# A hybrid decoder layer on one Trainium2 core: the squares of the delta-rule outputs are taken four chunks at a time and summed by VectorE, and VectorE makes the last square of the final norm

## The chip, the core and the metric

The kernel runs on one core of a Trainium2 chip. Five engines take part, each working through its own instruction queue in order: TensorE (PE in the profile: matrix products and transposes; PEld is its weight load, which overlaps), VectorE (DVE), ScalarE (ACT), GpSimd (POOL) and SyncE (SP, which here only issues transfers). The metric is the device time of one execution in microseconds. Three runs of the kernel before gave 1201.8, 1201.89 and 1199.36 us, median 1201.8; the profiled execution took 1200.36 us.

## The reference, cut to what matters

One layer of a decoder over 1024 tokens of width 1024, all in float32.

```python
h = rmsnorm(x, norm1_w)
proj = h @ w_in                       # q, k, v, z of mixer A; q, k, v of mixer B
...                                   # mixer A: short convolution, L2-normed q and k
def step(state, xs):                  # over chunks of tokens, for each of 4 heads
    uv, wk, qd, at, ke, ge = xs
    u = uv - wk @ state
    o = qd @ state + at @ u
    state = ge * state + ke.T @ u
    return state, o
o_a = rmsnorm(o_a, gdn_norm_w) * silu(z)      # mean square over the 128 columns of a head
o_b = dilated_attention(qb, kb, vb)           # mixer B, 8 heads of 64
x = x + concat(o_a, o_b) @ w_out
...                                   # rmsnorm, up projection, width-3 convolution, silu gate
x = x + (silu(gate) * up) @ w_down
return rmsnorm(x, final_norm_w)
```

The two things the change touches are the mean square in `rmsnorm(o_a, ...)` (one number for each token and head) and a quarter of the last eighth of the mean square in the final `rmsnorm`.

## The kernel before

**Stages.** The program is written as coroutines ("streams") that yield to a small planner, the class `Weave`. The planner keeps an estimated clock of TensorE and an estimated time at which every tile is ready, worked out from fixed costs for each engine (VectorE 0.07 us plus 0.00105 us an element, ScalarE 0.12 plus 0.00085, and 0.15 more for a square with an accumulated sum). At each point it lets the ready stream of the smallest level number go on. The order in which matrix products are emitted is the order on TensorE. On the other engines a list scheduler sets the order: operations issued through `uv` and `ua` (VectorE and ScalarE, recorded on line 144) go ahead of those issued through `ve` and `ac` (line 142). Line 193 is the helper that issues a matrix product, line 197 the one that issues a transpose.

In order of time the stages are: input projection of the keys; preparation of the four delta-rule heads; the four chains (about 240 to 305 us); the attention (about 320 to 442 us); the output projection; the MLP up (to about 800 us) and down (to about 1189 us); the final norm (to the end). The dense input projection, `dense`, is a stream of low rank that is cut into groups of three products of 128x512 (`ps<-xhi,whi`, `ps<-xlo,whi`, `ps<-xhi,wlo`: a float32 product made of three products of rounded parts). It supplies TensorE with work wherever the planner sees the chains or the attention not ready, and does so until after the attention. So a product of it that is done earlier is missing later, but none is lost.

**A chain.** `chain(h)` runs the recurrence of one head over 8 chunks of 128 tokens; four chains are interleaved. In each chunk: TensorE makes `kT` times the state `ct`; VectorE makes `r`; TensorE makes `yt` times `r` (`ps<-r,um`); VectorE scales it to `wke` and ScalarE copies it to `w`; TensorE makes `ps<-wke,ktok`; VectorE updates the state `ct`; TensorE makes the output `po` out of `ct,qat` and `w,qat`; ScalarE and then VectorE write the output into `vtok` (`vtok<-ps,rq`, `vtok<-ps,gq,vtok`). Before the change ScalarE then squares the chunk's 128x128 outputs into a scratch tile `osq` and adds the squares of each token up on the way into one column of `ms` (the accumulated sum is a second instruction, ACTIVATION_READ_ACCUMULATOR). After the 8 chunks VectorE scales `ms` to a mean, GpSimd takes its power of minus one half and scales `vtok` by it, and `finish(h)` transposes `vtok` and stores it through the tile `ot` for the gate. Tiles `ot`, and later tiles of the attention and of the norms, share a ring of two buffers, tag "t2".

**The end.** The last five steps of the down product for four output tiles are made in `last_product`, first for columns 0 to 255 ("left"), then 256 to 511 ("right"). After each, `add_to` adds the product to `x1h` (VectorE), and `complete` squares the 128x256 result on ScalarE; all squares but the very last (`apart`) are added into `rstdB` by VectorE. `mean_of` sums over partitions with products against a column of ones, first from `rstdB`, then from the last square `sq3` (`sq` in the profile); GpSimd takes the power; `turned` spreads it by a transpose; `scale_out` scales the tiles and stores them. The scaling of left tiles 6 and 7 is tied behind the last addition on VectorE by a manual dependency.

Of the kernel before, what the change touches and what calls it, by code (L numbers as in the profile page):

```python
# [7 lines left out]
F32 = mybir.dt.float32  # L8
F32R = mybir.dt.float32r
AF = mybir.ActivationFunctionType  # L10
OP = mybir.AluOpType
AX = mybir.AxisListType
# [3 lines left out]
P = 128  # L16
# [131 lines left out]
def hybrid_layer(tc, I, out):  # L148
    nc = tc.nc
    wv = Weave()  # L150
    ve = Engine(wv, nc.vector, "vector", 0.07, 0.00105)
    ac = Engine(wv, nc.scalar, "scalar", 0.12, 0.00085)

    uv = Engine(wv, nc.vector, "vector", 0.07, 0.00105, first=tc.high_priority)
    ua = Engine(wv, nc.scalar, "scalar", 0.12, 0.00085, first=tc.high_priority)
# [7 lines left out]
    sp = es.enter_context(tc.tile_pool(name="sp", bufs=1))  # L163
# [3 lines left out]
    def tile_(pool, shape, dt, name, tag, bufs):  # L167
        return wv.slot(pool.tile(list(shape), dt, name=name, tag=tag, bufs=bufs), tag, bufs)
# [3 lines left out]
    def A(name, tag, dt=F32, shape=(P, 1024)):  # L172
        if tag in TURNS:
            i = turns[tag] = turns.get(tag, -1) + 1
            tag = TURNS[tag][i % len(TURNS[tag])]
        return tile_(lp, shape, dt, name, tag, SLOTS[tag])
# [15 lines left out]
    def mm(dst, lhs, rhs, us, start=True, stop=True, **kw):  # L192
        tc.stamp_issue_order_token(nc.tensor.matmul(dst, lhs, rhs, start=start, stop=stop, **kw).ins, TOKEN)  # L193
        wv.product(us, dst, lhs, rhs)
# [54 lines left out]
    def rsqrt(dst, src, n):  # L249
        po_.tensor_tensor(dst, src, mhalf[:, :n], op=OP.pow)  # L250
# [14 lines left out]
    def bank(tag, name="ps"):  # L265
        return tile_(pp_, (P, 512), F32, name, tag, 2)

    def next_bank(tag, *tiles, slack=0.0):

        while max(wv.need(*tiles), wv.slot_free(tag, 2)) + slack > 1e-3:  # L270
            yield max(wv.need(*tiles), wv.slot_free(tag, 2)) + slack
        return bank(tag)

    def half(i):
        return slice(i * 512, i * 512 + 512)

    def v8(t):
        return t.rearrange("p (c t) -> p c t", c=NCH)
# [239 lines left out]
    def small(name, bufs=2):  # L518
        return tile_(sp, (P, NCH), F32, name, name, bufs)
# [316 lines left out]
    def chain_load(h, s):  # L836
        t = A("qat", "go" if s == 1 and h < 2 else "qa", shape=(P, 2, 512))
        sy.dma_start(t[:, 0, :], qpark[h][:, half(s)])
        sy.dma_start(t[:, 1, :], atpark[h][:, half(s)])
        return t  # L840
# [3 lines left out]
    def chain(h):  # L844

        for i in range(H):
            yield from wv.until(("m", i))
            yield from wv.until(("v", i))
        d = G[h]
        kT, ktok, vtok, yt, ge, rq, gq, ke = [d[n] for n in ("kT", "ktok", "vtok", "yt", "ge", "rq", "gq", "ke")]  # L850
        if not ct:
            ct.append(A("ct", "uy", shape=(P, 8, P)))
        sts = ct[0][:, 2 * h:2 * h + 2, :]
        qa = chain_load(h, 0)
        ps = bank(("asc", "ch")[h // 2])
        ms = small("ms", 4)
        tg = str(h)
        st = None
        for c in range(NCH):
            cs = slice(c * P, (c + 1) * P)  # L860
            if c == 2 and h < 2:
                qb = chain_load(h, 1)
            if c == 3 and h >= 2:
                yield from wv.until(("c", h - 2, 3))
                qb = chain_load(h, 1)
            if c == 4:
                qa = qb
            qT, at = [qa[:, i, (c % 4) * P:(c % 4 + 1) * P] for i in range(2)]
            if c == 0:
                r = vtok[:, cs]  # L870
                yield wv.need(ps, vtok, yt)
            else:
                yield wv.need(ps, st, slack=HOP)
                mm(ps[:, 0:P], kT[:, cs], st, 0.215)
                r = tile_(sp, [P, P], F32, "r", "r" + tg, 1)
                uv.scalar_tensor_tensor(r, ps[:, 0:P], ngam[:, c, h:h + 1], vtok[:, cs], op0=OP.mult, op1=OP.add)
                yield wv.need(r, slack=HOP)
            mm(ps[:, P:2 * P], yt[:, c, :], r, 0.215)
            w = tile_(sp, [P, P], F32, "w", "w" + tg, 1)
            if c < NCH - 1:  # L880
                wke = tile_(sp, [P, P], F32, "wke", "r" + tg, 1)
                uv.tensor_scalar(wke, ps[:, P:2 * P], ke[:, c:c + 1], None, op0=OP.mult)
            ua.activation(w, ps[:, P:2 * P], AF.Copy)
            if c < NCH - 1:
                yield wv.need(wke, slack=HOP)
                mm(ps[:, 2 * P:3 * P], ktok[:, cs], wke, 0.215)
                sn = sts[:, c % 2, :]
                if c == 0:
                    uv.tensor_copy(sn, ps[:, 2 * P:3 * P])
                else:  # L890
                    uv.scalar_tensor_tensor(sn, st, ge[:, c:c + 1], ps[:, 2 * P:3 * P], op0=OP.mult, op1=OP.add)
            yield wv.need(w, qa, slack=HOP)
            po = yield from next_bank("atr")
            if c:
                mm(po[:, P:2 * P], qT, st, 0.215)
            mm(po[:, :P], at, w, 0.215)

            ua.activation(vtok[:, cs], po[:, :P], AF.Copy, scale=rq[:, c:c + 1])
            if c:
                uv.scalar_tensor_tensor(vtok[:, cs], po[:, P:2 * P], gq[:, c:c + 1], vtok[:, cs], op0=OP.mult,  # L900
                                        op1=OP.add)
            if c < NCH - 1:
                st = sn
            osq = tile_(sp, [P, P], F32, "osq", "osq", 1)
            ua.activation(osq, vtok[:, cs], AF.Square, accum_out=ms[:, c:c + 1])
            wv.done.add(("c", h, c))

        ve.tensor_scalar(ms, ms, 1.0 / 128, EPS, op0=OP.mult, op1=OP.add)
        rsqrt(ms, ms, NCH)
        po_.tensor_tensor(v8(vtok), v8(vtok), ms[:, :, None].to_broadcast([P, NCH, P]), op=OP.mult)  # L910
        wv.add(1, finish(h, vtok))

    def finish(h, osb):
        for hh in range(2):
            pt = yield from next_bank("atr", osb)
            for c in range(4):
                i = 4 * hh + c
                tp(pt[:, c * P:(c + 1) * P], osb[:, i * P:(i + 1) * P])
            ot = tile_(sp, [P, 512], F32, "ot", "t2", 2)
            ac.activation(ot, pt, AF.Copy, scale=gw2)  # L920
            sy.dma_start(mixer[h][:, half(hh)], ot)
        wv.done.add(("o", h))
# [589 lines left out]
    def part(m, hh, sl):  # L1512
        return slice(512 * hh + sl.start, 512 * hh + sl.stop)
# [6 lines left out]
    def complete(m, hh, sl, apart=False):  # L1520

        sp_ = part(m, hh, sl)
        x = x1h[m][:, sp_]
        sq = tile_(sp, [P, 512], F32, "sq3", "t2", 2)
        ac.activation(sq[:, sl] if m else rstdB[:, sp_], x, AF.Square)
        if apart:
            return sq
        if m:
            ve.tensor_tensor(rstdB[:, sp_], rstdB[:, sp_], sq[:, sl], op=OP.add)

# [38 lines left out]
    def mlp_down():  # L1569
# [4 lines left out]
        def down_step(stage, j):  # L1574
            for e, (op, pds) in enumerate(zip(ops[stage, j], (pa, pb))):
                for i in range(4):
                    down(pds[i], i, op, whole, j == 0 and (stage == 0 or (stage, e) == (1, 1)), j == HT - 1)
                if j == HT - 1:
                    mg, hh = ADDS[stage][e]
                    for i in range(4):  # L1580
                        add_to(pds[i], 4 * mg + i, hh, whole)
                        if stage == 0 and e == 1:
                            complete(i, 0, whole)
                        if stage == 2 and e == 1:
                            complete(i, 1, whole)
                    if stage == 2 and e == 1:
                        for i in range(4):
                            complete(4 + i, 1, whole)
# [35 lines left out]
    for h in range(H):  # L1624
        wv.add(1, chain(h))
# [65 lines left out]
```

## Time and profile before

| | before |
|---|---|
| median of three runs | 1201.8 us |
| the profiled execution | 1200.36 us |
| its span, from first to last instruction | 1198.6 us |
| TensorE busy | 1187.5 us (99%) |
| VectorE busy | 915.1 us (76%) |
| ScalarE busy | 574.8 us (48%) |
| GpSimd busy | 89.8 us (7%) |
| mean granted TensorE clock | 0.997 |
| squares of the chains, ScalarE | 32 of 0.307 us, and 32 reads of the sum of 0.188 us |

A row of the timeline has the start in us from the start of the span, the duration in us, the engine, the line, the operation, written tile <- read tiles with shapes, and the count of merged instructions; in square brackets stands how long the engine had been idle before, and what ended that. A row of the waits has the waiting engine and tile, who was waited for, the us in total, how often, and the longest. A row of a group has count, total busy us and mean ns of one. A row of the windows has for each stretch its length and the busy us of each engine.

### The profile page before, as it was taken

How to read it: one execution, taken by the hardware profiler on the slowest of the kernel's cores; microseconds unless marked ns; L12 is line 12 of the kernel's file. 1: busy time of each engine (PE TensorE's matmuls, PEld its weight loads, DVE VectorE, ACT ScalarE, POOL GpSimd, SP SyncE). 2: the span in 40 equal slices, each digit the busy share in tenths (PEclk: the TensorE clock that was granted, in tenths of full speed). 3: DMA queues.
4: the chain of work that ended last, by engine and by line, in shares of the span. 5: the costliest groups of instructions: out<-in, count | busy, mean ns of one | idle time of the engine just before them, and what ended most of it. 6: DMA issues, size and time to landing. Idle time of an engine off the chain costs nothing.

```text
span 1198.6 us, 18324 instructions
## 1 busy us (share of the span) xinstructions
PE 1187.5 (99%) x7050; PEld 983.7 (82%) x7050; DVE 915.1 (76%) x1450; ACT 574.8 (48%) x1126; POOL 89.8 (7%) x100
## 2 busy tenths in 40 slices
PE   9999999999999999999999999999999999999997
PEld 7888888888777778888888888888888888888886
DVE  7683975665355566777989888989898889999875
ACT  7275345355454443655544544445445454434441
POOL 0212010214311120000000000000000000000000
PEclk9999999999999999999999999999999999999998
DMA  7435234436634204543213223131222398557414
GB/s 237 107 95 150 85 109 127 152 113 183 224 95 124 73 28 128 180 154 110 88 54 104 90 70 106 53 106 60 99 90 69 109 371 292 192 157 229 160 53 141
DMA packets 85798, 154.80 MB, mean 129 GB/s; under 512 B 21168, under 2 KB 36304, under 8 KB 85712
## 3 DMA queue, kind: packets, MB, share of 16 engines
q1 hardware_dynamic: 84848, 152.85, 39.1%
q8 instruction: 55, 0.90, 0.3%
q10 hardware_dynamic: 864, 0.79, 0.2%
q14 instruction: 31, 0.25, 0.1%
HBM read 117.68 MB, written 35.93 MB: 128 GB/s over the span
## 4 chain that ended last, share of the span: by engine, by line
PE 95%; DVE 2%; ACT 2%; issue 1%; DMA 0%; POOL 0%; POOLq 0%; DVEq 0%; SPq 0%; ACTq 0%
PE ps L193 45%; PE pa L193 20%; PE dw L193 17%; PE pc L193 10%; PE ps L197 3%; DVE kT L142 1%; ACT sm L144 0%; DMA xt<-in_xT 0%; DVE x1h L142 0%; ACT whi L142 0%; PE pd L193 0%; DVE zz L142 0%; ACT dec L142 0%; DVE xr L142 0%; DVE rstdB L142 0%
## 5 line engine op out<-in xcount | busy, mean ns | idle before, releaser
L193 PE MATMUL dw<-pr 128*128 128x512 f32 (+1 forms) x984 | 211.3, 376 | 0.0
L193 PEld LDWEIGHTS dw<-pr 128*128 128x128 f32 x984 | 176.7, 188 | 33.6
L193 PE MATMUL ps<-xhi,whi 128*128 128x512 f32 x384 | 157.7, 411 | 0.3 <-ACT xhi L144 0.3
L193 PE MATMUL ps<-xhi,wlo 128*128 128x512 f32 x384 | 150.3, 391 | 0.0
L193 PE MATMUL ps<-xlo,whi 128*128 128x512 f32 x384 | 148.4, 390 | 0.0
L193 PE MATMUL pa<-T,pair 128*128 128x512 f32 x528 | 127.0, 389 | 0.0
L193 PEld LDWEIGHTS pa<-T,pair 128*128 128x128 f32 x528 | 99.0, 188 | 20.6
L193 PEld LDWEIGHTS ps<-xhi,whi 128*128 128x128 f32 x384 | 72.5, 189 | 19.6 <-issue 5.6
L193 PEld LDWEIGHTS ps<-xhi,wlo 128*128 128x128 f32 x384 | 72.4, 188 | 15.7
L193 PEld LDWEIGHTS ps<-xlo,whi 128*128 128x128 f32 x384 | 72.3, 188 | 12.5
L142 ACT ACTIVATE u<-pa 128x512 f32<-128x512 f32 x44 | 26.3, 598 | 107.2 <-PE pa L193 107.2
L142 DVE SCALAR_TENSOR_TENSOR y<-xu,fcw,y 128x1023 f32<-128x1023 f32 (+1 forms) x44 | 56.4, 1281 | 22.1 <-ACT y L142 22.0
L142 ACT ACTIVATE whi<-wst 128x1024 fp32r<-128x1024 f32 x36 | 38.2, 1063 | 65.4 <-PE ps L193 54.3
L193 PE MATMUL pa<-B,A 128*128 128x512 f32 x264 | 63.4, 389 | 0.0
L193 PE MATMUL pa<-T,S 128*128 128x512 f32 x264 | 63.4, 389 | 0.0
L193 PE MATMUL pc<-B,pair 128*128 128x512 f32 x264 | 63.4, 389 | 0.0
L193 PE MATMUL pc<-T,S 128*128 128x512 f32 x264 | 63.4, 389 | 0.0
L142 DVE TENSOR_TENSOR wst<-wst 128x512 f32<-128x512 f32 x88 | 60.5, 688 | 0.9
L193 PE MATMUL ps<-B,pair 128*128 128x512 f32 x252 | 60.5, 389 | 0.0
L142 POOL TENSOR_TENSOR rs<-rs,mhalf 128x2 f32<-128x2 f32 (+2 forms) x4 | 4.7, 1187 | 738.4 <-DVE rs L144 738.4
L142 ACT ACTIVATE pr<-wd 128x1024 fp32r<-128x1024 f32 x33 | 34.9, 1058 | 49.5 <-PE dw L193 37.0
L144 ACT ACTIVATE sm<-sm,mx 128x128 f32<-128x128 f32 (+7 forms) x64 | 35.4, 556 | 48.2 <-DVE mx L144 48.2
(248 smaller groups left out, 2411.1 us busy)
## 6 DMA issues: line engine op xcount, KB each, us to landing
wst<-in_wu SPq DMA_DIRECT2D x44, 512.0 KB, 3.7
wd<-in_wd SPq DMA_DIRECT2D x44, 512.0 KB, 4.5
upark<-y SPq DMA_DIRECT2D x22, 512.0 KB, 3.6
wst<-in_wi SPq DMA_DIRECT2D x21, 512.0 KB, 3.8
r<-upark SPq DMA_DIRECT2D x11, 512.0 KB, 7.5
r<-upark SPq DMA_DIRECT2D x22, 256.0 KB, 7.5
wa<-in_wd SPq DMA_DIRECT2D x22, 256.0 KB, 3.3
wst<-in_wv SPq DMA_DIRECT2D x8, 512.0 KB, 3.7
```

The costliest lines, as they stand in the source:

```text
L142: return getattr(eng, op)(*a, **kw)
L144: return getattr(eng, op)(*a, **kw)
L193: tc.stamp_issue_order_token(nc.tensor.matmul(dst, lhs, rhs, start=start, stop=stop, **kw).ins, TOKEN)
L197: tc.stamp_issue_order_token(nc.tensor.transpose(dst, src, ident if idt is None else idt).ins, TOKEN)
```

## The change

The square of the chains' outputs is no longer made for each chunk. After chunks 3 and 7 ScalarE squares four chunks in one 128x512 instruction into a tile of the ring "t2", without accumulating, and VectorE reduces it along the 128 columns of each chunk into four columns of `ms`. Both are issued through the ordinary engines `ac` and `ve`, not the urgent ones. In the final norm, the last square (`apart`) is a product of the tile with itself on VectorE in place of a ScalarE square.

```diff
             if c < NCH - 1:
                 st = sn
-            osq = tile_(sp, [P, P], F32, "osq", "osq", 1)
-            ua.activation(osq, vtok[:, cs], AF.Square, accum_out=ms[:, c:c + 1])
+            if c % 4 == 3:
+                osq = tile_(sp, [P, 4, P], F32, "osq", "t2", 2)
+                hs = half(c // 4)
+                ac.activation(osq.rearrange("p c d -> p (c d)"), vtok[:, hs], AF.Square)
+                ve.tensor_reduce(out=ms[:, c - 3:c + 1], in_=osq, op=OP.add, axis=AX.X)
             wv.done.add(("c", h, c))
...
         sq = tile_(sp, [P, 512], F32, "sq3", "t2", 2)
+        if apart:
+            ve.tensor_tensor(sq[:, sl], x, x, op=OP.mult)
+            return sq
         ac.activation(sq[:, sl] if m else rstdB[:, sp_], x, AF.Square)
-        if apart:
-            return sq
         if m:
             ve.tensor_tensor(rstdB[:, sp_], rstdB[:, sp_], sq[:, sl], op=OP.add)
```

Since the planner's costs differ, the order moves from the middle of the chains to the end of the attention, and at the very end. The instructions of TensorE are the same, 6081, in another order. On VectorE, in the middle of the chains, the first of the eight reductions stands between an update of the states and the next output:

```order
 L144 SCALAR_TENSOR_TENSOR r<-ps,ngam,vtok 128x128
 L144 SCALAR_TENSOR_TENSOR ct<-ct,ge,ps 128x128 x2
+L142 TENSOR_REDUCE ms<-osq 128x4
 L144 SCALAR_TENSOR_TENSOR vtok<-ps,gq,vtok 128x128
 L144 TENSOR_SCALAR wke<-ps,ke 128x128
```

The reduction is now ahead of the `wke` that the next state of a chain needs. On TensorE, right behind the product that uses this `wke`, the planner now puts one more group of three dense products:

```order
 L193 MATMUL ps<-xhi,wlo 128x512
 L193 MATMUL ps<-wke,ktok 128x128
+L193 MATMUL ps<-xhi,whi 128x512
+L193 MATMUL ps<-xlo,whi 128x512
+L193 MATMUL ps<-xhi,wlo 128x512
 L193 MATMUL ps<-ct,qat 128x128
 L193 MATMUL ps<-w,qat 128x128
```

The output products `ct,qat` and `w,qat` moved behind that group. By the first transposes of the attention 15 dense products more are done than before, and a run of 45 dense products inside the attention has become one of 30; the other runs there keep their lengths. The conversions of the dense weights (`whi` on ScalarE, `wlo` on GpSimd) and the reads of finished dense banks (`aqkv` on VectorE) fall into other steps of the attention. At the very end VectorE's queue was, before:

```order
L142 TENSOR_TENSOR rstdB<-rstdB,sq_10777 128x256
L142 TENSOR_TENSOR x1h<-x1h,dw 128x256
L142 SCALAR_TENSOR_TENSOR x1h<-x1h,fw,ps 128x256 x2
L144 TENSOR_SCALAR rs_10811<-ps 128x2
L142 SCALAR_TENSOR_TENSOR x1h<-x1h,fw,ps 128x256 x8
```

and is now, at the same place:

```order
L142 TENSOR_TENSOR rstdB<-rstdB,sq_10737 128x256
L142 TENSOR_TENSOR x1h<-x1h,dw 128x256
L142 SCALAR_TENSOR_TENSOR x1h<-x1h,fw,ps 128x256 x2
L142 TENSOR_TENSOR sq_10760<-x1h 128x256
L144 TENSOR_SCALAR rs_10771<-ps 128x2
L142 SCALAR_TENSOR_TENSOR x1h<-x1h,fw,ps 128x256 x8
```

The square, which ScalarE made beside the two scalings, now stands behind them on VectorE.

## The prediction

> **What bounds the kernel now.** I read the busy times first, then the stretches of time, then what TensorE waited for in the stages that the change touches, then the timeline at those waits.
>
> ```profile
> span 1198.6 us, 18324 instructions
> PE 1187.5 (99%) x7050; PEld 983.7 (82%) x7050; DVE 915.1 (76%) x1450; ACT 574.8 (48%) x1126; POOL 89.8 (7%) x100
> ...
> 260.00:270.00 10.00, 10.00 (x82) 9.70 (x81) 8.51 (x30) 6.99 (x30) 0.30 (x1) 1.00 0.40 126
> 270.00:280.00 10.00, 9.53 (x75) 8.94 (x74) 7.74 (x28) 6.59 (x30) 0.35 (x1) 1.00 0.44 117
> ...
> 320.00:440.00 120.00, 119.61 (x1530) 92.81 (x1527) 70.96 (x243) 60.80 (x205) 23.55 (x45) 1.00 0.29 93
> ```
>
> The columns behind the length are the busy times of TensorE, its weight load, VectorE, ScalarE and GpSimd. TensorE is the bound: in the attention it lacks 0.4 us of 120, in the middle of the chains nothing in one stretch of ten and 0.47 us in the next. So ScalarE's 6.6 to 7.0 us of every ten there cannot be what the chains' stage costs. What TensorE waited for between 240 and 306 us is the most that any relief of another engine could bring there:
>
> ```profile
> PE ps L193 <- ACT w L144: 0.5, 1, 0.5
> PE ps L193 <- DVE ct L144: 0.5, 1, 0.5
> ```
>
> Two waits, 1.0 us. From 1190 us on TensorE has no product left that doesn't wait for another engine, and each delay there counts in full.
>
> **The chains.** ScalarE loses 32 squares and their 32 reads of the sum, and gains 8 squares of 128x512; VectorE gains 8 reductions of 128x512.
>
> ```profile
> L144 ACT ACTIVATE osq<-vtok x32: 293/310/312, 248.0 to 304.6; 128x128 f32<-128x128 f32 x32
> L144 ACT ACTIVATION_READ_ACCUMULATOR osq<-vtok x32: 185/187/192, 248.3 to 304.8; 128x1 f32 x32
> ```
>
> ```profile
> L142 ACT ACTIVATE sq<-x 128x512 f32<-128x512 f32 x14 | 8.7, 619 | 0.5 <-DVE rstdB L142 0.5
> ...
> L142 DVE TENSOR_TENSOR aqkv<-ps,rstdB 128x512 f32<-128x512 f32 x16 | 17.8, 1112 | 21.7 <-PE ps L193 21.7
> ...
> L144 DVE CUSTOM_DVE_ANT_0 sm<-ps,mk 128x448 f32<-128x448 f32 x8 | 4.7, 620 | 0.0
> ...
> L142 DVE COPY rstdB<-ps 128x512 f32<-128x512 f32 x4 | 2.7, 685 | 0.2 <-PE ps L197 0.2
> ```
>
> ScalarE: 32 x (0.310 + 0.187) = 15.9 us of instructions go, 8 x 0.619 = 5.0 come, so 10.9 us less. VectorE: no reduction of this form is in the trace. The nearest rows are a plain copy of 128x512 (0.685) and an operation of 448 elements that keeps an extreme as it goes (0.620); the dearest row of 128x512 is `aqkv`, which writes in another order than it reads (1.112). The reduction reads in order, so I take 0.69, with 0.62 and 1.11 as ends. That is 8 x 0.69 = 5.5 us more on VectorE (5.0 to 8.9), none of it on TensorE.
>
> Where does it lie? VectorE is 8.5 of ten us busy in the middle of the chains, and its queue is in order, so a reduction holds up the `wke`, `r` and `ct` behind it, and TensorE waits for those. The first one stands ahead of a `wke`. In the trace of before this is that `wke` and the product that uses it:
>
> ```profile
> 263.93 0.35 DVE L144 TENSOR_SCALAR wke<-ps,ke 128x128 f32<-128x128 f32 x1
> ...
> 264.35 0.48 PE L193 MATMUL ps<-xhi,whi 128*128 128x512 f32 x1
> 264.67 0.39 PE L193 MATMUL ps<-xlo,whi 128*128 128x512 f32 x1
> 264.90 0.40 PE L193 MATMUL ps<-xhi,wlo 128*128 128x512 f32 x1
> 265.14 0.39 PE L193 MATMUL ps<-wke,ktok 128*128 128x128 f32 x2
> ```
>
> `wke` was done at 264.28 and used at 265.14: a slack of 0.86 us, more than the 0.69. The dense group ahead is the cover. The group that the change adds behind that product takes 265.14 - 264.35 = 0.79 us of useful TensorE work that is missing later, and gives VectorE as much time to catch up. Breaking into dense work costs little: the first product of a group holds TensorE 264.67 - 264.35 = 0.32 us where the second holds it 0.23, so one more group is 0.1 us at most. Without that cover the price of a reduction is its whole 0.69.
>
> The wait for ScalarE is where a square stood ahead of two copies `w`:
>
> ```profile
> 272.34 0.72 DVE L144 TENSOR_SCALAR wke<-ps,ke 128x128 f32<-128x128 f32 x2
> ...
> 272.75 0.30 ACT L144 ACTIVATE osq<-vtok 128x128 f32<-128x128 f32 x1
> ...
> 273.04 0.43 ACT L144 ACTIVATE w<-ps 128x128 f32<-128x128 f32 x2
> ...
> 273.36 0.49 PE L193 MATMUL ps<-wke,ktok 128*128 128x128 f32 x2 [0.47 <-ACT w L144]
> ```
>
> The copy `w` could start 273.04 - 272.75 = 0.29 us earlier without that square. But the third reduction now stands in VectorE's queue a few operations ahead of these two `wke`, and pushes their start from 272.34 by up to 0.69: the wait is passed on from ScalarE to VectorE. I cost it at no change. The other wait, for `ct`, is behind a read of a dense bank on VectorE, which stays where it was.
>
> The new tiles share the ring "t2" with `ot`, which stays occupied until its store has landed.
>
> ```profile
> mixer<-ot SPq DMA_DIRECT2D x8, 256.0 KB, 4.4
> ```
>
> So a square of a second group of four chunks can wait on ScalarE for a store of 4.4 us, ahead of a `w`. In the new order the square of the third head is the one behind a store; between that `ot` and the square TensorE makes five products of the chains, six dense products and a set of transposes, some 3.5 us by the spacing of 0.23 for either kind in the rows above, and a dense group stands ahead of the product that uses the `w`. I cost it at nothing; the uncovered rest is up to about 1 us, once.
>
> So the chains' term is zero: between -1.0 (both waits gone) and +5.5 (every reduction wholly on TensorE's path).
>
> **The attention.** Its order on TensorE keeps its fillers but for 15 products taken earlier. What moves is which step the conversions `whi` and the bank reads `aqkv` fall into. In the trace of before one `whi` stood between two exponentials:
>
> ```profile
> 348.87 0.33 PEld L197 LDWEIGHTS ps<-ident,sm 64*128 64x128 f32 x8 [0.17 <-ACT whi L142]
> ...
> 349.41 0.20 PEld L197 LDWEIGHTS ps<-ident,sm 64*128 64x128 f32 x4 [0.22 <-ACT sm L144]
> ```
>
> It held the weight loads of the transposes, and with them TensorE, for 0.17 + 0.22 = 0.39 us. In ScalarE's order two `whi` stood so before, and two stand between exponentials now, of another step: no change taken. Bounds: -0.8 (neither costs anything) and +3.5 (nine such moved operations cost 0.39 each).
>
> **The end.** Here the change puts work on the path.
>
> ```profile
> 1188.99 0.42 DVE L142 TENSOR_TENSOR x1h<-x1h,dw 128x256 f32<-128x256 f32 x1
> ...
> 1189.33 0.87 DVE L142 SCALAR_TENSOR_TENSOR x1h<-x1h,fw,ps 128x256 f32<-128x256 f32 x2
> 1189.51 0.42 ACT L142 ACTIVATE sq<-x1h 128x256 f32<-128x256 f32 x1 [1.15 <-DVE x1h L142]
> 1189.97 0.52 PEld L193 LDWEIGHTS ps<-ones,sq 128*128 128x128 f32 x4 [0.37 <-ACT sq L142]
> ```
>
> ScalarE squared at 1189.51 to 1189.93 beside VectorE's two scalings, and TensorE went on 0.04 us later. Now the square stands behind the scalings, which end at 1190.20; an instruction of this queue starts about 0.08 us before the one ahead ends (1189.33 against 1188.99 + 0.42). So it runs from 1190.12 for the 0.42 of the same-sized addition to 1190.54, and TensorE goes on at 1190.58: 0.61 us later. If it starts only at 1190.20 it is 0.69. What follows (the power, the transpose, eight scalings, the stores) is one chain and moves with it: +0.65. The ends are 0.61 and, if the square cost as much as a scaling more (0.87 / 2), 1.1.
>
> **Sum.** 0 + 0 + 0.65 = about +0.7 us on the profiled execution's 1200.36, so 1201.1. The median of the runs is 1.4 above that execution; on it I forecast 1202.5. A difference of 0.2% (2.4 us) is about what a measurement of this kernel can tell from no change, and the forecast lies within.
>
> **Rivals.** First, slower: VectorE becomes the bound of the chains. For it speaks 8.51 of ten us busy, against it the slack of 0.86. It decides once the slack ahead of the reductions is below their 0.69 at most of the eight places: 5.5 + 0.7 = +6.2, 1208.0; at half of them +3.5, 1205.3. The Trainium skill (VectorE: DVE Perf Modes, "Rules for kernel authors") speaks for this one: a reduction on a hot path runs at one element a cycle and is called the slowest operation of that engine. By that page's 0.96 GHz, 512 elements would be an estimate of 0.53 us each, 4.3 for eight, and this rival 1206.8 in place of 1208.0; no reduction is in the trace to compare.
>
> Second, slower: the attention, TensorE-bound to 0.4 us in 120, meets its moved conversions at worse places: +3.5 + 0.7, 1206.0.
>
> Third, the relief counts: both waits of the chains vanish and the reductions hide, -1.0 + 0.7 = -0.3, 1201.5. This is still within 0.2%; for more, TensorE had to lose time that its waits don't show.
>
> **Chances.** The forecast 0.56, the third rival 0.11; the first 0.15, the second 0.11; gains that I can't place 0.07. So within 0.2%: 0.67; slower 0.26; faster 0.07. The forecast's own range is 1201.4 to 1203.8. The range over the cases goes down to 1199.9, which the runs' own spread of 2.5 us asks for, and up to 1205.8, half of the first rival.
>
> **What would show it.** Right: eight TENSOR_REDUCE of 0.6 to 0.7 us, eight squares of 0.62; TensorE's waits between 240 and 306 us again near 1 us; TensorE reaching the products against `sq` 0.6 us later behind the last down product, with VectorE as what it waited for. Wrong: TensorE waits for `wke`, `r` or `ct` of several times 0.5 us (first rival), waits for `sm` or for banks (second), or a shorter time from the first to the last chain product with no wait at all (third). A reduction much over 0.7 us would break the chains' term first.

## The result, and the profile after

The changed kernel takes 1202.95 us (median of 14 runs, 1201.99 to 1204.15); the kernel before, run beside it, 1200.38 us (14 runs, 1199.36 to 1201.89). The ratio is 1.0021, with a 95% interval of 1.0013 to 1.0028: slower by 2.6 us, just over the 0.2% of the prediction. The time lies 0.45 us over the forecast of 1202.5, but that stood on a median of before of 1201.8 (three runs): the difference is +2.6 us in place of +0.7.

The head of the page of the changed kernel, with the busy times:

```profile
span 1200.7 us, 18300 instructions
PE 1186.7 (99%) x7050; PEld 982.5 (82%) x7050; DVE 919.0 (77%) x1459; ACT 568.5 (47%) x1069; POOL 89.3 (7%) x100
```

Three stretches of its time (length, then busy us of TensorE, its weight load, VectorE, ScalarE, GpSimd):

```profile
260.00:270.00 10.00, 10.00 (x78) 9.27 (x77) 8.64 (x30) 5.37 (x16) 0.30 (x1) 1.00 0.34 107
270.00:280.00 10.00, 9.57 (x74) 8.86 (x73) 8.35 (x29) 4.97 (x16) 0.00 (x0) 1.00 0.36 104
320.00:440.00 120.00, 119.77 (x1533) 92.95 (x1532) 70.70 (x243) 62.59 (x206) 23.27 (x45) 1.00 0.29 96
```

In the middle of the chains ScalarE is busy 5.0 to 5.4 of ten us where it was 6.6 to 7.0, VectorE 0.1 and 0.6 more than before, and TensorE as full as before. The attention has lost nothing. The new instructions cost what was forecast (count, then ns least, median, most):

```profile
L142 ACT ACTIVATE osq<-vtok x8: 622/632/637, 261.9 to 308.1; 128x512 f32<-128x512 f32 x8
L142 DVE TENSOR_REDUCE ms<-osq x8: 652/684/687, 262.9 to 308.7; 128x4 f32<-128x512 f32 x8
```

TensorE's waits between 240 and 330 us have a new first line:

```profile
PE ps L197 <- POOL vtok L142: 1.2, 2, 1.0
PE ps L193 <- DVE ct L144: 0.4, 1, 0.4
PE ps L193 <- ACT w L144: 0.4, 1, 0.4
```

The two waits of before are still there, 0.1 us shorter each by these rounded figures. New are two, together 1.2 us, for GpSimd's scaling of `vtok`: the transposes of the third head's output wait 0.3 us, those of the fourth 1.0. What led there is in the timeline of the fourth head. Before, from the last chunk's output to the transposes:

```profile
304.20 0.32 DVE L144 SCALAR_TENSOR_TENSOR vtok<-ps,gq,vtok 128x128 f32<-128x128 f32 x1
304.56 0.31 ACT L144 ACTIVATE osq<-vtok 128x128 f32<-128x128 f32 x1 [0.48 <-DVE vtok L144]
304.99 0.17 DVE L142 TENSOR_SCALAR ms<-ms 128x8 f32<-128x8 f32 x1 [0.47 <-ACT osq L144]
305.31 1.64 POOL L142 TENSOR_TENSOR ms<-ms,mhalf 128x8 f32<-128x8 f32 x1 [1.22 <-DVE ms L142]
307.02 1.90 POOL L142 TENSOR_TENSOR vtok<-vtok,ms 128x1024 f32<-128x1024 f32 x1
310.17 2.38 POOL L142 TENSOR_TENSOR wlo<-wst,whi 128x1024 fp32r<-128x1024 f32 x1 [1.25 <-ACT whi L142]
311.04 1.04 PE L197 MATMUL ps<-ident,vtok 128*128 128x128 f32 x8
```

And in the changed kernel:

```profile
307.57 0.35 DVE L144 SCALAR_TENSOR_TENSOR vtok<-ps,gq,vtok 128x128 f32<-128x128 f32 x1 [3.49 <-ACT vtok L144]
308.06 0.63 ACT L142 ACTIVATE osq<-vtok 128x512 f32<-128x512 f32 x1 [0.52 <-DMA mixer<-ot]
308.72 0.69 DVE L142 TENSOR_REDUCE ms<-osq 128x4 f32<-128x512 f32 x1 [0.80 <-ACT osq L142]
309.33 1.11 DVE L142 TENSOR_TENSOR aqkv<-ps,rstdB 128x512 f32<-128x512 f32 x1
310.26 2.41 POOL L142 TENSOR_TENSOR wlo<-wst,whi 128x1024 fp32r<-128x1024 f32 x1 [2.71 <-ACT whi L142]
310.27 0.17 DVE L142 TENSOR_SCALAR ms<-ms 128x8 f32<-128x8 f32 x1
312.63 1.64 POOL L142 TENSOR_TENSOR ms<-ms,mhalf 128x8 f32<-128x8 f32 x1
314.35 1.90 POOL L142 TENSOR_TENSOR vtok<-vtok,ms 128x1024 f32<-128x1024 f32 x1
316.29 1.09 PE L197 MATMUL ps<-ident,vtok 128*128 128x128 f32 x8 [0.96 <-POOL vtok L142]
```

Before, the power started 305.31 - 304.52 = 0.79 us after the last output was done; now 312.63 - 307.92 = 4.71 us. The square and its sum take 1.5 us of that (307.92 to 309.41), a read of a dense bank that stands ahead of `ms` on VectorE 0.9, `ms` 0.2, and the rest of GpSimd's residual `wlo` (the part of a dense weight that its rounding to `whi` leaves over), which now stands ahead of the power, 2.2. Before, the scaling was done at 308.92 and used at 311.04, a slack of 2.1 us; the start is 3.9 us later, dense products placed ahead of the transposes cover a part of the difference, and 1.0 us is left over. GpSimd's order in the two programs, ahead of the attention (before, then after; third head from the first `ms`, fourth from the second):

```
 TENSOR_TENSOR ms<-ms,mhalf 128x8            TENSOR_TENSOR ms<-ms,mhalf 128x8
 TENSOR_TENSOR vtok<-vtok,ms 128x1024        TENSOR_TENSOR wlo<-wst,whi 128x1024
 TENSOR_TENSOR wlo<-wst,whi 128x1024         TENSOR_TENSOR vtok<-vtok,ms 128x1024
 MEMSET pb                                   MEMSET pb
 TENSOR_TENSOR ms<-ms,mhalf 128x8            TENSOR_TENSOR wlo<-wst,whi 128x1024
 TENSOR_TENSOR vtok<-vtok,ms 128x1024        TENSOR_TENSOR ms<-ms,mhalf 128x8
 TENSOR_TENSOR wlo<-wst,whi 128x1024         TENSOR_TENSOR vtok<-vtok,ms 128x1024
```

The end of the changed kernel, from the last sum of a down bank to the products against `sq`:

```profile
1190.21 0.42 DVE L142 TENSOR_TENSOR x1h<-x1h,dw 128x256 f32<-128x256 f32 x1
...
1190.55 0.86 DVE L142 SCALAR_TENSOR_TENSOR x1h<-x1h,fw,ps 128x256 f32<-128x256 f32 x2
1191.34 0.42 DVE L142 TENSOR_TENSOR sq<-x1h 128x256 f32<-128x256 f32 x1
1191.81 0.52 PEld L193 LDWEIGHTS ps<-ones,sq 128*128 128x128 f32 x4 [0.98 <-DVE sq L142]
```

From the last sum to these products it is 1191.81 - 1190.21 = 1.60 us; before it was 1189.97 - 1188.99 = 0.98.

To compare stages across executions I take three marks in each trace: the second copy `ct` on VectorE (start of the chains), the 34th conversion `whi` on ScalarE (behind the attention), and the last power `rs` on GpSimd, this against the last sum of a down bank. The lengths in us between them, for the kernels of the next section too (the last two ran once each and are read for single instructions only; their stages of 204.64 and 204.68 are those of the change to 0.2):

| kernel | chains and attention | last sum to last power | ratio to before (95%) |
|---|---|---|---|
| before | 203.05 | 1.94 | |
| the change | 204.46 | 2.55 | 1.0021 (1.0013 to 1.0028) |
| final square alone | 203.11 | 2.55 | 1.0004 (0.9995 to 1.0013) |
| chains alone | 204.49 | 1.94 | 1.0015 (1.0006 to 1.0024) |
| GpSimd's order mended | 202.94 | 2.55 | 1.0006 (0.9997 to 1.0015) |
| final square first | 205.01 | 1.89 | 1.0021 (1.0011 to 1.0031) |
| own ring | 203.72 | 2.55 | 1.0013 (1.0004 to 1.0022) |
| own ring, order mended | 202.96 | 2.55 | 1.0007 (0.9998 to 1.0016) |
| order mended, reductions twice | 203.69 | 2.55 | 1.0010 (1.0001 to 1.0019) |
| all three | 202.93 | 1.89 | 1.0002 (0.9993 to 1.0011) |

The change costs 204.46 - 203.05 = 1.41 us in the chains and 2.55 - 1.94 = 0.61 at the end, 2.0 in sum. Its profiled execution lost a further 0.5 us in the output projection, to a load of `x` that landed late; no other execution has that load as late, with the same order there, so I put it down to that execution (two others lose as much further on, in the MLP). The median is 2.6 us slower; its interval, about 0.9 us to either side, takes in the 2.0. The intervals of the other kernels are about 1.1 us to either side: the ratios say which group a kernel belongs to, and differences of half a us are read from the traces.

### The profile page after: what moved, and what is told of

It reads as the page before. It is cut to its first block, busy times and chain, and to the rows that moved or that the text cites. A ratio compares the mean times of both kernels' runs of the same rounds, so it can differ in the third digit from the quotient of the medians.

```text
span 1200.7 us, 18300 instructions
## 1 busy us (share of the span) xinstructions
PE 1186.7 (99%) x7050; PEld 982.5 (82%) x7050; DVE 919.0 (77%) x1459; ACT 568.5 (47%) x1069; POOL 89.3 (7%) x100
## 4 chain that ended last, share of the span: by engine, by line
PE 71%; DVE 1%; issue 1%; DMA 1%; ACT 0%; POOLq 0%; POOL 0%; DVEq 0%; ACTq 0%
PE ps L193 22%; PE pa L193 20%; PE dw L193 17%; PE pc L193 10%; PE ps L197 2%; DMA x<-in_xT 1%; DVE x1h L142 0%; PE pd L193 0%; DVE zz L142 0%; ACT sm L144 0%; DVE rstdB L142 0%; ACT hb L142 0%; ACT rstdB L142 0%; DVE pt L144 0%; POOLq L1691 0%
## 5 line engine op out<-in xcount | busy, mean ns | idle before, releaser
L193 PEld LDWEIGHTS pc<-B,pair 128*128 128x128 f32 x264 | 49.5, 188 | 10.3
L193 PEld LDWEIGHTS pa<-B,A 128*128 128x128 f32 x264 | 49.6, 188 | 10.3
```

## The experiments

**The final square alone.** The kernel before, with the second part of the change only:

```diff
         sq = tile_(sp, [P, 512], F32, "sq3", "t2", 2)
+        if apart:
+            ve.tensor_tensor(sq[:, sl], x, x, op=OP.mult)
+            return sq
         ac.activation(sq[:, sl] if m else rstdB[:, sp_], x, AF.Square)
-        if apart:
-            return sq
```

> Only the last square of the final norm is made by VectorE; the chains are as before, and so is every order up to the end. If each part of the change costs what its waits show: the products against `sq` start 0.6 to 0.7 us later behind the last down product than before (before 0.90 us from the last sum of a down bank to the products, now 1.60), and the time is before + 0.6 (ratio 1.0005). If the end alone made the change slower, it is before + 2.1 (1.0018).

Measured: 1.0004, and 0.61 us more from the last sum to the power, as expected if each part costs what its waits show. (The 0.90 us of before in the expectation is 0.98 in the trace.)

**The chains alone.** The kernel before, with the first part of the change only:

```diff
-            osq = tile_(sp, [P, P], F32, "osq", "osq", 1)
-            ua.activation(osq, vtok[:, cs], AF.Square, accum_out=ms[:, c:c + 1])
+            if c % 4 == 3:
+                osq = tile_(sp, [P, 4, P], F32, "osq", "t2", 2)
...
+                ve.tensor_reduce(out=ms[:, c - 3:c + 1], in_=osq, op=OP.add, axis=AX.X)
```

> Only the chains' squares are taken four chunks at a time and summed by VectorE; the end is as before. The order of every queue up to the end is that of the changed kernel. If the chains' part costs what TensorE waits for there more than before (waits of 0.3 and 1.0 us for GpSimd's scaling of `vtok`, those for `ct` and `w` 0.2 us shorter, one more group of dense products broken into): before + 1.2 to 1.4 (ratio 1.0011). If the late load of `x` in the output projection (0.5 us in the changed kernel's profile) also belongs to it: + 1.8. If the chains cost nothing, as forecast: 1.0000.

Measured: 1.0015 and 1.44 us more in the stage, with the same waits for `vtok`, 0.3 and 1.0; the output projection took what it took before. The two parts add up, and seven tenths of the 2.0 us lie in the chains, where the forecast had zero. Here the last square started 0.04 us behind its input and waited for no store, and the waits for `vtok` are the same, so the store in the ring `t2` is not what makes them.

**GpSimd's order mended.** The changed kernel, with the residuals ordered behind the scalings; TensorE's, VectorE's and ScalarE's orders are unchanged by it (two pairs of DMA issues on SP change places):

```diff
-            po_.tensor_tensor(lo, st, hi.bitcast(F32), op=OP.subtract)
+            plo = po_.tensor_tensor(lo, st, hi.bitcast(F32), op=OP.subtract)
+            if "norm" in last:
+                after(plo, last["norm"])
...
-        po_.tensor_tensor(v8(vtok), v8(vtok), ms[:, :, None].to_broadcast([P, NCH, P]), op=OP.mult)
+        last["norm"] = po_.tensor_tensor(v8(vtok), v8(vtok), ms[:, :, None].to_broadcast([P, NCH, P]), op=OP.mult)
```

> The changed kernel, but GpSimd makes the residuals `wlo` of the two dense weights behind the scalings of `vtok` of the third and fourth head, as it did before, and no longer ahead of them; TensorE's, VectorE's and ScalarE's orders are those of the changed kernel. If GpSimd's order is the cause: TensorE's waits of 0.3 and 1.0 us for `vtok` shrink to 0.2 or less, and the time is 1.1 to 1.3 us under the changed kernel's (ratio to before 1.0010). If the reductions on VectorE or the moved products are the cause, nothing changes: 1.0021. If the residual, now 2 to 5 us later, makes the next dense products wait, that is a new wait for `wlo` on GpSimd, up to 1 us.

Measured: 1.0006, and the stage takes 202.94 us, 1.52 less than in the changed kernel and 0.11 less than before. No wait for `vtok` is left:

```profile
PE ps L193 <- DVE ct L144: 0.4, 1, 0.4
PE ps L193 <- ACT w L144: 0.4, 1, 0.4
```

```profile
310.70 0.63 ACT L142 ACTIVATE osq<-vtok 128x512 f32<-128x512 f32 x1 [1.44 <-DMA mixer<-ot]
...
313.23 1.64 POOL L142 TENSOR_TENSOR ms<-ms,mhalf 128x8 f32<-128x8 f32 x1 [3.96 <-DVE ms L142]
314.95 1.90 POOL L142 TENSOR_TENSOR vtok<-vtok,ms 128x1024 f32<-128x1024 f32 x1
316.80 2.39 POOL L142 TENSOR_TENSOR wlo<-wst,whi 128x1024 fp32r<-128x1024 f32 x1
316.90 1.09 PE L197 MATMUL ps<-ident,vtok 128*128 128x128 f32 x8
```

That is the place of the loss: with VectorE's eight reductions and the moved products in the same order, it goes when two residuals change places with the scalings. With the same order on TensorE, the two programs can be set side by side product by product: they part by 0.5 us at the third head's transposes and by 1.0 at the fourth's, and nowhere else in the stage by over 0.05. The later residual made nothing wait. In this execution the last square had waited for a store, 0.9 us longer than in the changed kernel's, and the scaling (done at 316.85) was in time by less than 0.1 us; the mended order left just that much.

**The final square first.** The changed kernel, with the last two scalings ordered behind the square:

```diff
-            ve.tensor_tensor(sq[:, sl], x, x, op=OP.mult)
+            last["square"] = ve.tensor_tensor(sq[:, sl], x, x, op=OP.mult)
...
-        scale_out(0, left, pl, range(6, 8), anchor=fourth)
+        scale_out(0, left, pl, range(6, 8), anchor=last["square"])
```

> The changed kernel, but the last square stands ahead of the two scalings that it was behind on VectorE. If its place is what costs 0.6 to 0.7 us and not the engine: the products against `sq` start 0.8 us earlier than in the changed kernel, 0.1 to 0.2 earlier than before, and the time is 0.8 under the changed kernel's (ratio to before 1.0014). If a square on VectorE is dear wherever it stands, no gain. If the two scalings, now behind it, hold the next step `rs` on VectorE: the gain is under 0.4.

Measured: 1.0021, no gain in the time, although the end is as short as expected:

```profile
1192.73 0.42 DVE L142 TENSOR_TENSOR x1h<-x1h,dw 128x256 f32<-128x256 f32 x1
...
1193.19 0.42 DVE L142 TENSOR_TENSOR sq<-x1h 128x256 f32<-128x256 f32 x1
1193.53 0.86 DVE L142 SCALAR_TENSOR_TENSOR x1h<-x1h,fw,ps 128x256 f32<-128x256 f32 x2
1193.67 0.52 PEld L193 LDWEIGHTS ps<-ones,sq 128*128 128x128 f32 x4 [0.32 <-DVE sq L142]
```

The products against `sq` stand 0.94 us behind the last sum, 0.66 earlier than in the changed kernel, though only 0.04 earlier than before (0.1 to 0.2 were expected): the square needs the sum's result and starts 0.46 us after the sum did, where the scaling, which needs nothing of it, started 0.34 after. What the end gained, the chains of the profiled execution lost: 205.01 against 204.46 us, with a last wait for `vtok` of 1.5 us. Its last square had waited for a store (1.42 us against 0.52):

```profile
311.46 0.63 ACT L142 ACTIVATE osq<-vtok 128x512 f32<-128x512 f32 x1 [1.42 <-DMA mixer<-ot]
...
313.18 2.40 POOL L142 TENSOR_TENSOR wlo<-wst,whi 128x1024 fp32r<-128x1024 f32 x1 [3.13 <-ACT whi L142]
...
313.67 1.93 DVE L142 TENSOR_SCALAR ms<-ms 128x8 f32<-128x8 f32 x1
```

One execution, the second slowest of nine, doesn't explain a median; the interval takes in the 1.0014 that was expected, and the same edit, made where the chains don't wait, does gain (all three, below). Why the median here shows nothing stays open.

**An own ring for the squares.** The changed kernel with the squares out of `t2`:

```diff
-                osq = tile_(sp, [P, 4, P], F32, "osq", "t2", 2)
+                osq = tile_(sp, [P, 4, P], F32, "osq", "osq", 1)
```

> The changed kernel, but the squares of four chunks have a ring of their own with one buffer in place of a turn in `t2`, so they no longer wait for a store of `ot`. GpSimd's order changes with it: the power of the fourth head comes ahead of the residual `wlo`, its scaling of `vtok` still behind; the third head's two stand ahead. If GpSimd's place in line is the cause: the wait for `vtok` at the third head is gone (0.3), that at the fourth is 0.3 to 0.5 us in place of 1.0 to 1.5, together 0.8 to 1.2 under the changed kernel (ratio to before 1.0013). If the store's landing is the cause, the last square starts within 0.2 us of its input and both waits are gone: 1.0010. If neither: 1.0021.

This edit also moves a few operations on the other engines and a few dense products. On GpSimd, as the expectation says, the third head's scaling now stands ahead of its residual and the fourth head's power ahead of the next one; only the fourth head's scaling is still behind a residual.

Measured: 1.0013, the stage 203.72 us. The last square now starts with its input, the third head's wait is gone, and the fourth's is half:

```profile
PE ps L197 <- POOL vtok L142: 0.5, 1, 0.5
```

That is what GpSimd's order makes of it: the scaling of the fourth head waits for a residual of 2.4 us. The store is not the cause, or this wait would be gone too.

**Both mended.** The two edits above in one kernel, own ring and GpSimd's order.

> The changed kernel with both: the squares' own ring, and the residuals behind the scalings on GpSimd. If the late store only matters through the slack of the last scaling: no wait for `vtok`, and the time is that of the kernel with GpSimd's order alone to 0.3 us (ratio to before 1.0005). If the store's wait costs by itself: 0.5 to 1.0 us under that one (1.0000).

Measured: 1.0007 and 202.96 us, the same as with GpSimd's order alone. In these two executions the wait for the store in `t2` cost nothing, since GpSimd took the power and the scaling at once.

**The reductions twice.** GpSimd's order mended, and a second reduction behind each, written past the planner's account so that TensorE's order stays:

```diff
                 ve.tensor_reduce(out=ms[:, c - 3:c + 1], in_=osq, op=OP.add, axis=AX.X)
+                nc.vector.tensor_reduce(out=ms[:, c - 3:c + 1], in_=osq, op=OP.add, axis=AX.X)
```

> The kernel with GpSimd's order mended, and each of the eight reductions made twice (the second writes the same sums), so 8 x 0.69 = 5.5 us more on VectorE; TensorE's order is the same. If the reductions lie beside TensorE's work, as forecast: the time is that of the kernel without the doubling plus at most 0.7 us, for the last one ahead of the last scaling (ratio to before 1.0006 to 1.0012), and the waits for `ct` and `w` stay near 0.4 each. If VectorE bounds the chains: 3 to 5.5 us more (1.003 to 1.005), with waits for `wke`, `r` or `ct`.

Measured: 1.0010, and 203.69 us in the stage, 0.75 more than without the doubling:

```profile
L911 DVE TENSOR_REDUCE ms<-osq x8: 643/679/686, 264.6 to 310.7; 128x4 f32<-128x512 f32 x8
```

Eight times 0.68, 5.4 us, cost 0.75. TensorE's list of waits is that of the mended kernel (0.4 for `ct`, 0.4 for `w`), but its weight loads wait more for the state `ct` on VectorE. The first line is of this kernel from 266 to 290 us, the second of the kernel without the doubling from 268 to 292 us, the same place in its stage:

```profile
PEld ps L193 <- DVE ct L144: 0.9, 4, 0.3
PEld ps L193 <- DVE ct L144: 0.2, 1, 0.2
```

The 0.7 us between them are nearly the whole loss. (A few operations of VectorE and ScalarE changed places too, so a part can be theirs.) So the first rival, the reductions on TensorE's path, does not hold at one set of reductions; at two, VectorE begins to hold TensorE, for a seventh of the 5.4 us added.

**All three.** Both mended, with one set of reductions, and the final square ahead of the two scalings.

> All three: own ring, GpSimd's order, and the last square ahead of the two scalings on VectorE. If the changed kernel's loss is these places in line and nothing else: no wait for `vtok`, the products against `sq` at the same distance from the last sum as before, and the time is before - 0.2 to + 0.2 (ratio 1.0000). If something else of the change costs, what is left over 1.0003 is its price.

Measured: 1.0002, 202.93 us in the chains, 1.89 at the end. With the three places in line mended, the change's instructions cost nothing that can be measured, and bring nothing either: the stage is 203.05 - 202.93 = 0.12 us shorter. That is ScalarE's relief and VectorE's reductions together; no run separates the two. None of the kernels beats the one before.

**A late square, and another form of `ms`.** In the kernel with the square first the step `ms` took 1.93 us in place of 0.17. Two kernels, run once each, ask why. The changed kernel, with its last square made three times so that `ms` falls into GpSimd's residual; in the second kernel `ms` is also made in another form, with a tile of constants:

```diff
                 ac.activation(osq.rearrange("p c d -> p (c d)"), vtok[:, hs], AF.Square)
+                if (h, c) == (3, 7):
+                    for _ in range(2):
+                        nc.scalar.activation(osq.rearrange("p c d -> p (c d)"), vtok[:, hs], AF.Square)
...
-        ve.tensor_scalar(ms, ms, 1.0 / 128, EPS, op0=OP.mult, op1=OP.add)
+        ve.scalar_tensor_tensor(ms, ms, 1.0 / 128, epsc, op0=OP.mult, op1=OP.add)
```

> The changed kernel, but the last square of the fourth head is made three times over on ScalarE, so that its sum is late and the step `ms` on VectorE (a TENSOR_SCALAR of 128x8, 0.17 us when alone) falls into GpSimd's residual `wlo` of 2.4 us. If GpSimd's work holds that step up, as the 1.93 us in the kernel with the square first suggests: it takes until `wlo` ends, some 1 us, and the power starts 0.1 to 0.3 us behind `wlo`. If the 1.93 us was a wait on something else: 0.17 us.

> As the one with the late square, but `ms` is made as SCALAR_TENSOR_TENSOR (a scale and the addition of a tile of constants) in place of TENSOR_SCALAR. If the hold depends on the form of VectorE's instruction: 0.2 us or less here, and the power starts at once behind `wlo`. If GpSimd holds every instruction of VectorE: some 1 us as in the other.

Measured, in the first of the two kernels:

```profile
310.25 2.39 POOL L142 TENSOR_TENSOR wlo<-wst,whi 128x1024 fp32r<-128x1024 f32 x1 [2.79 <-ACT whi L142]
...
310.67 0.69 DVE L142 TENSOR_REDUCE ms<-osq 128x4 f32<-128x512 f32 x1 [0.38 <-ACT osq L910]
311.39 1.27 DVE L142 TENSOR_SCALAR ms<-ms 128x8 f32<-128x8 f32 x1
```

and in the second:

```profile
310.58 2.39 POOL L142 TENSOR_TENSOR wlo<-wst,whi 128x1024 fp32r<-128x1024 f32 x1 [2.79 <-ACT whi L142]
...
311.72 1.28 DVE L142 SCALAR_TENSOR_TENSOR ms<-ms,epsc 128x8 f32<-128x8 f32 x1
```

Both end 0.02 to 0.03 us behind the residual (312.66 against 312.64, 313.00 against 312.97), so GpSimd's instruction holds them, in the one form as in the other. The reduction between them, 0.69 us inside the residual, is not.

## Why the prediction was right or wrong

The time fell into the forecast's range of 1201.4 to 1203.8 by luck. The difference was forecast at +0.7 us and came out at +2.6; what closed the gap is that the three runs of before had a median 1.4 us above that of the fourteen. Put on 1200.38, the same sum gives about 1201.1 and a range up to 1202.4, and 1202.95 lies outside it. Term by term:

- **The price of a reduction**, 0.69 (0.62 to 1.11): right, 0.684. The estimate of 0.53 under the first rival was too low by 0.15.
- **The relief of ScalarE**, 10.9 us: mis-sized, without effect. Its busy time fell by 6.3 us. Mostly that is overlap: a square and the read of its sum overlap (a square of before started at 300.19 for 0.30, its read at 300.39), and I had added them as if one followed the other. VectorE's busy time rose by 3.9 us, not 5.5, partly for the same reason.
- **The chains' term, zero.** This is the step that failed: +1.41 us. What it was argued from held, in sum. The reductions lie beside TensorE's work (GpSimd's order mended, 202.94 us against 203.05 before; doubled, still only +0.75), and the two waits of before came back at 0.4 each. But the sum followed a late result only to those who read VectorE's and ScalarE's queues. It did not follow the new square and its reduction to the step that they feed: `ms`, the power and the scaling on GpSimd, the transposes. The trace of before gave that chain a slack of 2.1 us, and the order of GpSimd's queue, which the working never followed, had a residual of 2.4 us moved ahead of it at both of the last heads. With the two residuals behind the scalings again, 1.52 us of the stage came back.
- **The wait in the ring `t2`**, costed at nothing with up to 1 us uncovered: right as far as it goes. It occurred, at the fourth head's last square and not at the third head's that was named (the square started 0.1 us behind its input in the changed kernel, 1.0 in the kernels with GpSimd's order mended and with the square first). In the first of these two it was covered, by less than 0.1 us; in the second it lay on the path.
- **The attention, zero**: right. Its stretch is as full as before and its wait for `sm` is 0.2 us, as before.
- **The end, +0.65 (0.61 to 1.1)**: right, +0.61; the square started 0.07 us before the scalings ended.
- **The rivals.** The first (VectorE bounds the chains, +3.5 to +6.2) falls with the doubled reductions. The second (conversions at worse places in the attention) had the right kind of mechanism, a moved conversion in the way, on the wrong engine and stage: it was the residual on GpSimd, ahead of the attention. The third (the relief counts, -1.0) comes to -0.1, net of the reductions. None of the cases that were given a chance had a slower time by GpSimd's queue.

## What to carry to other kernels

When a change makes a result later, follow that result to its last reader, through every queue that it crosses, the least busy engine's among them: GpSimd is busy 7% of the span here, and two instructions that changed places on it cost 1.5 us of the 2.0. Where an order is planned, compare the orders of all engines and set each moved instruction against the slack of what now stands behind it. And relieving an engine that is hardly waited for brings little: 6 us less of ScalarE, for 4 us more of VectorE, brought 0.1.

## What the runs showed of the hardware

A tiny step on VectorE, `ms` of 128x8, takes 0.17 us alone, and 1.93, 1.27 and 1.28 us where it started 0.5 to 1.1 us into a residual on GpSimd; it ends with that instruction, whichever of the two forms it has, while a reduction of 128x512 passes at its usual 0.69. In the changed kernel a `ms` that started 0.01 us behind a residual was not held (0.17). The Trainium skill (SBUF — State Buffer, "SBUF: two separate sides") says that VectorE and GpSimd share a pair of ports as an exclusive lock for whole instructions, and that VectorE's operations in a 2-port mode, or with two inputs from SBUF against a GpSimd operation that reads SBUF, take it. The traces agree for the residuals, which read SBUF: both forms of `ms` read SBUF alone and are held (the other form, with its tile of constants, has two inputs there), and the reduction, with one input and 0.69 us, is not. They don't agree for GpSimd's power: in the changed kernel a step of VectorE with two inputs, `vT<-xr,gcw,vT` of 128x1021, keeps its 1.28 us from 141.31 on, beside the power `rq<-ssq,mhalf` (141.16 to 142.90), while one of 128x1023 takes 2.14 beside a residual, and 1.28 elsewhere.

A part of the spread between executions lies ahead of the chains: the first `rst` starts on VectorE at 38.35 to 40.93 us in the twelve executions (two beyond 40.6, ten up to 39.2), and nine of them keep their distance up to the second copy `ct` within 0.1 us (202.7 us later). What delays the start was not tried.
